# RWKV preparation: both heads of a pair in one vector operation, pair products and transposes on quarters of the TensorE array

## The chip, the cores and the metric

The kernel runs on one core of one Trainium2 chip. The metric is the device time of one execution in microseconds (us), lower is better. The time before is the median of three runs. One further execution was profiled; all rows below come from it. "ns" is said where nanoseconds are meant.

## What is computed

One layer of a streaming encoder over 512 tokens of width 1024, in fp32: a pre-norm, one combined input projection `w_in`, two mixers side by side (an RWKV-7 mixer with 8 heads of 64 channels and a gated delta-rule mixer, GDN, with 4 heads of 128), sigmoid gates, an output projection, and a gated MLP of 2816 channels with a short causal convolution. The part around the change is the RWKV mixer. Its recurrence, per head and token, is

```python
sa = jnp.einsum('bhvk,bhk->bhv', S, a_t)
S = S * w_t[:, :, None, :] + sa[..., None] * b_t[:, :, None, :] + v_t[..., None] * k_t[:, :, None, :]
y = jnp.einsum('bhvk,bhk->bhv', S, r_t)
```

The kernel does it in chunks of 64 tokens. With decayed factors a, r (from the left) and b, k (from the right) of a chunk, it needs for each head and chunk the four products b·a, b·r, k·a, k·r, each 64 by 64 and masked to the lower triangle, and b and k themselves turned from channels-by-tokens to tokens-by-channels.

## The kernel before

Activations lie as channels on 128 partitions and 512 tokens in the free direction. A dense projection is done per unit of 128 output columns: `unit` loads 512 KB of weights, ACT writes their rounded part `hi` (line 161), DVE or POOL the remainder `lo` (line 163), and `mm3` issues three matmuls for each of the 8 input blocks (lines 176, 177, 179). These are called dense matmuls below; there are 24 in a unit.

`mixing` walks the list `ORDER`. `R0` to `R3` prepare the RWKV heads in pairs (`rwkv_prep`, head pair hp: head 2hp on partitions 0 to 63, called lo, head 2hp+1 on 64 to 127, called hi). `i0`, `i1` invert the triangular matrices of two pairs (`rwkv_inverse`), `c0`, `c1` run their chunks (`rwkv_chain`, `rwkv_out`). `a`, `G`, `z`, `I`, `C` are the same for GDN. `g0` to `g13` are dense gate projections that depend on nothing but the normalized input. The order of `ORDER` is a priority: a scheduler (tile pools, semaphores and the order on each engine are made by it when the program is built) takes on each engine the first piece of work that it believes to be ready. On the chip every engine then runs its own list strictly in that order.

`rwkv_prep` forms the decays `ep`, `em`, then on DVE:

- lines 470 and 472 write a and r: the lo half into the tile `ase`, the hi half into `aso`, each for all 8 chunks (64 partitions x 512);
- lines 486 and 491 write b and k into two tiles `BK`, one for each half of the sequence (4 chunks), per head and half: 4 + 4 operations of 64 partitions x 256. For the lo head b lies in slot 0 and k in slot 1, for the hi head the other way round;
- line 493 forms r·k·r_k, line 495 sums it on PE ("bones" matmul), line 496 makes `yf` of it.

Then, for each half of the sequence, three PSUM banks are taken (`pe`, `po`, `pt`). Lines 505 and 506 multiply, per chunk, the 64 rows of one head against [a r] into all 128 columns: the lo head into `pe`, the hi head into `po`. fp32 matmuls are issued twice, so a call in the code is two instructions in the trace. Line 508 transposes `BK` on the whole array into `pt`. DVE masks the products out of PSUM (line 512, four operations of 64 partitions x 512 for each half) into `ntb`, `ase`, `aso`; ACT copies `pt` (line 515); DVE scales `ntb` (line 516).

All PSUM tiles named `A` come out of one ring of 3 banks (`bank`, `BANKS`): the fourth `A` waits until the first has been read. `A` serves line 495, the products, the transposes, and several others.

`rwkv_inverse` begins on PE with line 569, after the last of 64 dependent DVE operations and the transpose of line 547.

## Time and profile before

| | |
|---|---|
| median of 3 runs | 902.66 us (899.92 to 904.11) |
| profiled execution | 901.19 us |
| its span, first to last instruction | 899.4 us |
| PE busy | 866.2 us, 96% |
| DVE busy | 590.1 us, 66% |
| ACT, POOL busy | 464.0 us, 195.4 us |
| granted TensorE clock | 0.992 of full speed |

The profile names an instruction by line, engine and operation, with the tiles that it writes and reads (`R` is the tile that holds `ase`, `aso`, `ntb`, `bkt`; `A`, `B`, `D` are PSUM banks; `P`, `T` work tiles). PE is the matrix engine, DVE the vector engine, ACT the scalar engine. A matmul's recorded duration includes the pipeline behind it; how fast PE proceeds is read from the distance of two starts. The first 48 us load inputs and form the first tiles, the mixing stage lies between some 48 and 433 us, projections and the MLP fill the rest.

### The profile page before, as it was taken

How to read it: one execution, taken by the hardware profiler on the slowest of the kernel's cores; microseconds unless marked ns; L12 is line 12 of the kernel's file. 1: busy time of each engine (PE TensorE's matmuls, PEld its weight loads, DVE VectorE, ACT ScalarE, POOL GpSimd, SP SyncE). 2: the span in 40 equal slices, each digit the busy share in tenths (PEclk: the TensorE clock that was granted, in tenths of full speed). 3: DMA queues.
4: the chain of work that ended last, by engine and by line, in shares of the span. 5: the costliest groups of instructions: out<-in, count | busy, mean ns of one | idle time of the engine just before them, and what ended most of it. 6: DMA issues, size and time to landing. Idle time of an engine off the chain costs nothing.

```text
span 899.4 us, 13124 instructions
## 1 busy us (share of the span) xinstructions
PE 866.2 (96%) x4925; PEld 675.9 (75%) x4925; DVE 590.1 (66%) x1156; ACT 464.0 (52%) x879; POOL 195.4 (22%) x182
## 2 busy tenths in 40 slices
PE   7998999999999999999999999999999999999995
PEld 4776777666767777677787888888888888888885
DVE  6799797874888987855486448766666666312125
ACT  7654457667443776583534464444444444323233
POOL 2241123111121221111222213222222222222221
PEclk8999999999999999999999999999999999999998
DMA  6331222121212221135252223332223333223234
GB/s 238 119 105 60 71 71 72 48 72 48 71 59 71 71 72 36 60 113 181 94 188 94 94 76 111 95 94 94 94 94 94 99 103 96 88 88 105 89 106 136
DMA packets 28737, 84.76 MB, mean 94 GB/s; under 512 B 3200, under 2 KB 5376, under 8 KB 28672
## 3 DMA queue, kind: packets, MB, share of 16 engines
q1 hardware_dynamic: 28672, 83.91, 29.3%
q8 instruction: 39, 0.64, 0.3%
q14 instruction: 26, 0.21, 0.1%
HBM read 78.13 MB, written 5.77 MB: 93 GB/s over the span
## 4 chain that ended last, share of the span: by engine, by line
PE 73%; DVE 16%; ACT 4%; issue 3%; DMA 2%; POOL 1%; SPq 0%; DVEq 0%; POOLq 0%; ACTq 0%
PE D L179 20%; PE D L176 20%; PE D L177 20%; DVE R L512 1%; PE A L176 1%; PE A L177 1%; PE A L179 1%; DVE invN L541 1%; DVE lo L163 1%; DVE P L747 1%; DMA raw<-w_in 1%; DVE invY L543 1%; ACT hi L161 1%; DVE R L926 1%; PE B L639 1%
## 5 line engine op out<-in xcount | busy, mean ns | idle before, releaser
L163 POOL TENSOR_TENSOR lo<-raw,hi 128x512 fp32r<-128x512 f32 x133 | 179.8, 1352 | 649.7 <-ACT hi L161 625.8
L161 ACT ACTIVATE hi<-raw 128x512 fp32r<-128x512 f32 (+1 forms) x266 | 165.0, 622 | 257.3 <-PE D L179 193.5
L176 PE MATMUL D<-uh,lo 128*128 128x512 f32 (+1 forms) x456 | 184.0, 405 | 2.7 <-ACT uh L200 1.9
L177 PE MATMUL D<-uh,hi 128*128 128x512 f32 (+1 forms) x456 | 184.1, 405 | 0.0
L163 DVE TENSOR_TENSOR lo<-raw,hi 128x512 fp32r<-128x512 f32 (+1 forms) x133 | 92.4, 695 | 77.2 <-ACT hi L161 76.8
L176 PE MATMUL D<-u2h,lo 128*128 128x512 f32 x352 | 137.9, 392 | 0.0
L177 PE MATMUL D<-u2h,hi 128*128 128x512 f32 x352 | 137.8, 392 | 0.0
L179 PE MATMUL D<-ul,hi 128*128 128x512 f32 (+1 forms) x456 | 135.4, 403 | 0.4 <-DVE ul L198 0.4
L176 PEld LDWEIGHTS D<-uh,lo 128*128 128x128 f32 x456 | 86.2, 189 | 23.5 <-ACT uh L200 2.4
L177 PEld LDWEIGHTS D<-uh,hi 128*128 128x128 f32 x456 | 86.1, 189 | 18.8 <-issue 1.0
L179 PEld LDWEIGHTS D<-ul,hi 128*128 128x128 f32 x456 | 82.6, 188 | 19.6 <-issue 1.2
L179 PE MATMUL D<-u2l,hi 128*128 128x512 f32 x352 | 95.1, 392 | 0.0
L177 PEld LDWEIGHTS D<-u2h,hi 128*128 128x128 f32 x352 | 66.1, 188 | 14.9 <-issue 0.2
L176 PEld LDWEIGHTS D<-u2h,lo 128*128 128x128 f32 x352 | 66.1, 188 | 14.7 <-issue 0.2
L179 PEld LDWEIGHTS D<-u2l,hi 128*128 128x128 f32 x352 | 66.1, 188 | 14.1
L972 DVE SCALAR_TENSOR_TENSOR P<-T,vecs,P 128x511 f32<-128x511 f32 x88 | 69.0, 784 | 8.9 <-ACT P L970 2.8
L969 DVE TENSOR_TENSOR T<-D,acc 128x512 f32<-128x512 f32 x44 | 30.3, 690 | 49.8 <-PE D L179 45.8
L177 PE MATMUL D<-ah,hi 128*128 128x512 f32 (+1 forms) x126 | 45.2, 366 | 0.0
L176 PE MATMUL D<-ah,lo 128*128 128x512 f32 (+1 forms) x126 | 45.1, 366 | 0.0
L541 DVE TENSOR_TENSOR invN<-invA,invY 128x60 f32<-128x60 f32 (+24 forms) x124 | 33.2, 268 | 2.6
L543 DVE TENSOR_TENSOR invY<-invY,invN 128x60 f32<-128x60 f32 (+24 forms) x124 | 32.9, 266 | 2.9
L970 ACT ACTIVATE P<-T,vecs 128x512 f32<-128x512 f32 x44 | 31.8, 723 | 5.4 <-DVE T L969 1.9
(342 smaller groups left out, 1280.1 us busy)
## 6 DMA issues: line engine op xcount, KB each, us to landing
raw<-w_in SPq DMA_DIRECT2D x44, 512.0 KB, 3.6
raw<-ffn_up SPq DMA_DIRECT2D x44, 512.0 KB, 3.5
raw<-ffn_down SPq DMA_DIRECT2D x18, 512.0 KB, 3.5
raw<-w_out SPq DMA_DIRECT2D x8, 512.0 KB, 3.5
spill<-T SPq DMA_DIRECT2D x14, 256.0 KB, 2.0
R<-spill SPq DMA_DIRECT2D x14, 256.0 KB, 5.6
raw<-ffn_down SPq DMA_DIRECT2D x9, 384.0 KB, 3.0
xin<-xT SPq DMA_DIRECT2D x8, 256.0 KB, 5.7
```

The lines of the kernel that those rows point to most:

```text
L161: nc.scalar.activation(hi[:, 0:w], raw[:, o:o + w], AF.Copy)
L163: self.on(str(self.halves % 4)).tensor_tensor(out=lo[:, 0:w], in0=raw[:, o:o + w], in1=hi[:, 0:w].bitcast(F32), op=ALU.subtract)
L176: nc.tensor.matmul(ps, wl[:, w[k]], x[k][0], start=(first and i == 0 and k == 0), stop=False)
L177: nc.tensor.matmul(ps, wh[:, w[k]], x[k][0], start=False, stop=False)
L179: nc.tensor.matmul(ps, wh[:, w[k]], x[k][1], start=False, stop=(last and i == len(parts) - 1 and k == n - 1))
L512: nc.vector.tensor_tensor(out=tl[s, w].rearrange("p c s t -> p c (s t)"), in0=ps[s, :].rearrange("p (c t) -> p c t", c=4), in1=rwm[s].unsq ...
L541: nc.vector.tensor_tensor(out=w, in0=rows[:, t, 0:t].unsqueeze(2).broadcast_to([128, t, n]), in1=Ym[:, t, c:G].unsqueeze(1).broadcast_to([ ...
L543: nc.vector.tensor_tensor(out=Ym[:, 0:t, c:G], in0=Ym[:, 0:t, c:G], in1=w, op=ALU.add)
L639: nc.tensor.matmul(pz[lo, 0, i, :], R[hp]["ase"][:, c, 0, :], se[:, i, 0, :], start=True, stop=True)
L969: nc.vector.tensor_tensor(out=h, in0=ps, in1=self.acc2, op=ALU.mult)
L970: nc.scalar.activation(cv, h, AF.Copy, scale=w(2))
L972: nc.vector.scalar_tensor_tensor(out=cv[:, sh:], in0=h[:, 0:T - sh], scalar=w(2 - sh), in1=cv[:, sh:], op0=ALU.mult, op1=ALU.add)
```

## The change

In `rwkv_prep` alone (two other places follow the new shape of the `BK` buffer, which is one tile of double size now in place of two):

- a and r are written for both heads by one operation each, into `ase` on all 128 partitions. ACT copies the hi half into `aso` afterwards, in two pieces.
- b and k are written for both heads and all 8 chunks by one operation each, b in slot 0 and k in slot 1 for both heads.
- A product is split into quarters of the array: 64 rows of one head against [a r] into 64 columns. Per chunk there are four: lo and hi head with b into the bank `pn` (lo into partitions 0 to 63, hi into 64 to 127), lo and hi head with k into the bank `pq` (halves crossed). The two banks thus hold roles (all b products, all k products), not heads, and two heads write one bank.
- `pn` is masked by one operation of 128 partitions, `pq` by two of 64: three for each half of the sequence, not four.
- The transposes are fp32 matmuls of a quarter against a 64 by 64 identity, 32 calls for 8 of before, at the end, into two banks for the whole sequence.

```diff
-        zero = self.work.tile([128, T], BF16, tag="BK", name="zero", bufs=2)
+        zero = self.work.tile([128, 2 * T], F32, tag="BK", name="zero", bufs=1).bitcast(BF16)[:, 0:T]
...
-        for tl, s in ((ase, slice(0, 64)), (aso, slice(64, 128))):
-            nc.vector.scalar_tensor_tensor(out=tl[s, :, 0, :], in0=kv[s], scalar=self.nkk[s, hp:hp + 1], in1=ep[s, :, 0:64],
-                                           op0=ALU.mult, op1=ALU.mult)
-            self.on("e").tensor_tensor(out=tl[s, :, 1, :], in0=rv[s], in1=ep[s, :, 1:65], op=ALU.mult)
+        lo, hi = slice(0, 64), slice(64, 128)
+
+        nc.vector.scalar_tensor_tensor(out=ase[:, :, 0, :], in0=kv, scalar=self.nkk[:, hp:hp + 1], in1=ep[:, :, 0:64],
+                                       op0=ALU.mult, op1=ALU.mult)
+        self.on("e").tensor_tensor(out=ase[:, :, 1, :], in0=rv, in1=ep[:, :, 1:65], op=ALU.mult)
+        for h in range(2):
+            nc.scalar.activation(aso[hi, 4 * h:4 * h + 4], ase[hi, 4 * h:4 * h + 4], AF.Copy)
...
-        bkh = [self.work.tile([128, 4, 2, 64], F32, tag="BK", name=self.nm("BK"), bufs=2) for _ in range(2)]
-        q = lambda x, s, h: x[s, h * 256:h * 256 + 256].rearrange("p (c t) -> p c t", c=4)
-        for h in range(2):
-            for s, sb in ((slice(0, 64), 0), (slice(64, 128), 1)):
-                nc.vector.scalar_tensor_tensor(out=bkh[h][s, :, sb, :], in0=q(K, s, h), scalar=self.hkk[s, hp:hp + 1],
-                                               in1=q(at, s, h), op0=ALU.mult, op1=ALU.mult)
+        bk = self.work.tile([128, 8, 2, 64], F32, tag="BK", name=self.nm("BK"), bufs=1)
+        c8 = lambda x: x.rearrange("p (c t) -> p c t", c=8)
+        nc.vector.scalar_tensor_tensor(out=bk[:, :, 0, :], in0=kv, scalar=self.hkk[:, hp:hp + 1], in1=c8(at),
+                                       op0=ALU.mult, op1=ALU.mult)
         self.on("b").tensor_tensor(out=K, in0=K, in1=tha, op=ALU.mult)
-        for h in range(2):
-            for s, sk in ((slice(0, 64), 1), (slice(64, 128), 0)):
-                self.on("c").tensor_tensor(out=bkh[h][s, :, sk, :], in0=q(K, s, h), in1=q(em, s, h), op=ALU.mult)
+        self.on("c").tensor_tensor(out=bk[:, :, 1, :], in0=kv, in1=c8(em), op=ALU.mult)
...
+        ident = self.con("ident")
+        quarters = ((lo, lo, 0), (hi, hi, 0), (lo, hi, 1), (hi, lo, 1))
         for h in range(2):
-            pe, po, pt = self.bank(), self.bank(), self.bank()
+            pn, pq = self.bank(), self.bank()
             for c in range(4):
...
-                nc.tensor.matmul(pe[:, o], bk[0:64], ase[0:64, cc].rearrange("p s t -> p (s t)"), start=True, stop=True)
-                nc.tensor.matmul(po[:, o], bk[64:128], aso[64:128, cc].rearrange("p s t -> p (s t)"), start=True, stop=True)
-            for c in range(4):
-                nc.tensor.transpose(pt[:, c * 128:c * 128 + 128], bkh[h][:, c, :, :].rearrange("p s t -> p (s t)"), self.con("ident"))
+                cc, o = 4 * h + c, slice(c * 128, c * 128 + 128)
+                for r_, w_, sl in quarters:
+                    nc.tensor.matmul((pn, pq)[sl][w_, o], bk[r_, cc, sl, :], ase[r_, cc].rearrange("p s t -> p (s t)"),
+                                     start=True, stop=True)
             w = slice(4 * h, 4 * h + 4)
-            for ps, s, tl in ((pe, lo, ntb), (pe, hi, ase), (po, hi, ntb), (po, lo, aso)):
+            for ps, s, tl in ((pn, slice(0, 128), ntb), (pq, hi, ase), (pq, lo, aso)):
...
-            nc.scalar.activation(bkt[:, w, :], pt.rearrange("p (c t) -> p c t", c=4), AF.Copy)
+        pt = [self.bank() for _ in range(2)]
+        for c in range(8):
+            for r_, w_, sl in quarters:
+                f = r_.start
+                nc.tensor.matmul(pt[f // 64][w_, c * 64:c * 64 + 64], bk[r_, c, sl, :], ident[r_, f:f + 64], start=True, stop=True)
+        for i in range(2):
+            nc.scalar.activation(bkt[:, :, 64 * i:64 * i + 64], c8(pt[i]), AF.Copy)
```

In the changed kernel the masks stand on line 511, the transposes on 518, the products on 507, the factors on 472, 474, 488 and 491; later lines move by 5.

The scheduler lays out the mixing stage anew. Three places follow, first before, then with the change.

PE at R0's products. In these rows `A_..` are the banks of the ring (the first number), `BK_..` the b/k tile, `R_27` the pair's `ase` or `aso`, `D_..` rows dense matmuls. Before:

```order
L179 MATMUL D_105_654<-ul_76,hi_103_650 128x512 x4
L495 MATMUL A_78_523<-P_29_277,cons_70 128x512
L505 MATMUL A_79_526<-R_27_275,BK_76_511 128x128
L506 MATMUL A_80_527<-R_27_275,BK_76_511 128x128
...
L176 MATMUL D_130_785<-uh_75,lo_127_778 128x512
L177 MATMUL D_130_785<-uh_75,hi_126_777 128x512
L176 MATMUL D_130_785<-uh_75,lo_127_778 128x512
L508 MATMUL A_81_528<-cons_70,BK_76_511 128x128 x4
...
L505 MATMUL A_82_546<-R_27_275,BK_77_512 128x128
L506 MATMUL A_83_547<-R_27_275,BK_77_512 128x128
...
L508 MATMUL A_84_548<-cons_70,BK_77_512 128x128 x4
```

With the change:

```order
L177 MATMUL D_104_685<-uh_75,hi_102_681 128x512
L495 MATMUL A_77_516<-P_29_277,cons_70 128x512
L507 MATMUL A_78_519<-R_27_275,BK_76_511 64x128 x2
L507 MATMUL A_79_520<-R_27_275,BK_76_511 64x128 x2
...
L507 MATMUL A_80_540<-R_27_275,BK_76_511 64x128 x5
L507 MATMUL A_81_541<-R_27_275,BK_76_511 64x128 x4
...
L518 MATMUL A_82_561<-cons_70,BK_76_511 64x64 x9
L518 MATMUL A_83_562<-cons_70,BK_76_511 64x64 x9
...
L176 MATMUL D_104_685<-uh_75,lo_103_682 128x512
```

Line 495 moved ahead of 8 dense matmuls of its unit; no dense matmul stands any more between it and the last transpose (before, 7 did in R0, 4 in R1 and R2, 2 in R3). `A_81` is the fourth ring bank after `A_78`, `A_82` after `A_79`, `A_83` after `A_80`.

DVE in R0, from the b/k factors to the masks. Before:

```order
L486 SCALAR_TENSOR_TENSOR BK_76_511<-P_28_276,sp_245,T_75_508 64x4x64 x2
L163 TENSOR_TENSOR lo_129_782<-raw_125_775,hi_128_781 128x512
L486 SCALAR_TENSOR_TENSOR BK_77_512<-P_28_276,sp_245,T_75_508 64x4x64 x2
L488 TENSOR_TENSOR P_28_276<-P_28_276,T_74_506 128x512
L491 TENSOR_TENSOR BK_76_511<-P_28_276,T_70_484 64x4x64 x2
L491 TENSOR_TENSOR BK_77_512<-P_28_276,T_70_484 64x4x64 x2
L493 SCALAR_TENSOR_TENSOR P_29_277<-P_29_277,vecs_69,P_28_276 128x512
...
L496 TENSOR_TENSOR yf_80<-A_78_523,R_27_275 128x512
L512 TENSOR_TENSOR R_27_275<-A_79_526,cons_70 64x512 x2
L512 TENSOR_TENSOR R_27_275<-A_80_527,cons_70 64x512 x2
```

With the change:

```order
L488 SCALAR_TENSOR_TENSOR BK_76_511<-P_28_276,sp_245,T_75_508 128x8x64
L163 TENSOR_TENSOR lo_127_844<-raw_123_837,hi_126_843 128x512
L490 TENSOR_TENSOR P_28_276<-P_28_276,T_74_506 128x512
L491 TENSOR_TENSOR BK_76_511<-P_28_276,T_70_484 128x8x64
L493 SCALAR_TENSOR_TENSOR P_29_277<-P_29_277,vecs_69,P_28_276 128x512
L351 SCALAR_TENSOR_TENSOR P_86_600<-D_98_648,vecs_69,P_86_600 128x511
L496 TENSOR_TENSOR yf_80<-A_77_516,R_27_275 128x512
L511 TENSOR_TENSOR R_27_275<-A_78_519,cons_70 128x512
L511 TENSOR_TENSOR R_27_275<-A_79_520,cons_70 64x512 x2
L511 TENSOR_TENSOR R_27_275<-A_80_540,cons_70 128x512
L511 TENSOR_TENSOR R_27_275<-A_81_541,cons_70 64x512 x2
```

Eight operations on b and k became two, the masks of `pn` are one operation, and the masks follow `yf` without a stop, in the order in which PE wants the banks back.

PE at the first matmul of the first inverse, i0 (`G_190` is the tile of G1, `G_153` with the change that of G0). Before:

```order
L770 MATMUL A_208_1390<-cons_70,G_190_1301 128x128 x4
...
L176 MATMUL D_230_1504<-uh_75,lo_229_1501 128x512
L177 MATMUL D_230_1504<-uh_75,hi_228_1500 128x512
L569 MATMUL B_153_1028<-invA_151_950,R_27_275 32x32 x16
L569 MATMUL B_153_1028<-invA_151_950,R_85_567 32x32 x16
```

With the change (lines moved by 5):

```order
L791 MATMUL A_182_1320<-cons_70,T_181_1318 128x128 x4
L803 MATMUL A_185_1334<-G_153_1170 128x128 x3
L574 MATMUL B_151_1090<-invA_149_1012,R_27_275 32x32 x16
L574 MATMUL B_151_1090<-invA_149_1012,R_84_598 32x32 x16
L803 MATMUL A_185_1334<-G_153_1170 128x128
```

The inverse's first matmul stood behind the transposes of G1 (line 770) and stands inside G0's preparation now: 448 dense matmuls of the program are ahead of it before, 378 with the change. The DVE operations of G1 that stood ahead of it went behind it.

## Rows read from the trace of the kernel before

**Rows 1.** The page: the span, the busy time of each engine, and the chain of work that ended last, by engine.

```profile
span 899.4 us, 13124 instructions
PE 866.2 (96%) x4925; PEld 675.9 (75%) x4925; DVE 590.1 (66%) x1156; ACT 464.0 (52%) x879; POOL 195.4 (22%) x182
PE 73%; DVE 16%; ACT 4%; issue 3%; DMA 2%; POOL 1%; SPq 0%; DVEq 0%; POOLq 0%; ACTq 0%
```

**Rows 2.** Busy time by stretches: 20 us with a preparation (R1), 2 us out of them, and 20 us in the MLP. Columns: stretch, its length, busy us (and count) of PE, weight loads, DVE, ACT, POOL, then granted clock, DMA share, GB/s.

```profile
80.00:100.00 20.00, 18.71 (x100) 14.04 (x99) 16.84 (x29) 8.11 (x15) 3.61 (x5) 0.91 0.24 79
...
86.00:88.00 2.00, 2.00 (x6) 1.62 (x5) 1.92 (x6) 1.45 (x3) 0.18 (x1) 0.50 0.26 102
...
540.00:560.00 20.00, 20.00 (x89) 16.39 (x89) 17.40 (x22) 8.88 (x16) 5.79 (x4) 1.00 0.31 96
```

**Rows 3.** The waits of PE: which instruction waited for which, us in total, times, longest.

```profile
PE A L495 <- DVE P L493: 3.2, 3, 1.9
PE A L770 <- DVE G L751: 1.5, 2, 1.0
PE B L651 <- ACT SUV L648: 1.5, 3, 0.7
PE A L460 <- ACT T L456: 1.1, 1, 1.1
PE A L799 <- ACT T L793: 1.0, 2, 0.6
PE B L569 <- DVE invA L547: 1.0, 2, 0.8
PE A L786 <- POOL T L783: 0.9, 1, 0.9
PE B L881 <- DVE st L895: 0.9, 1, 0.9
PE B L576 <- ACT invY L572: 0.8, 1, 0.8
```

**Rows 4.** Instructions grouped by line and shape: out and in, shapes, count, busy us, mean ns of one, idle time before them.

```profile
L470 DVE SCALAR_TENSOR_TENSOR R<-P,sp,Ep 64x512 f32<-64x512 f32 x8 | 6.2, 772 | 2.0 <-ACT Ep L450 1.9
L472 DVE TENSOR_TENSOR R<-P,Ep 64x512 f32<-64x512 f32 x8 | 5.7, 710 | 0.0
L486 DVE SCALAR_TENSOR_TENSOR BK<-P,sp,T 64x256 f32<-64x256 f32 x16 | 8.6, 540 | 0.2
L491 DVE TENSOR_TENSOR BK<-P,T 64x256 f32<-64x256 f32 x16 | 8.7, 544 | 0.2
L512 DVE TENSOR_TENSOR R<-A,cons 64x512 f32<-64x512 f32 x32 | 21.1, 686 | 1.4 <-PE A L506 1.1
L493 DVE SCALAR_TENSOR_TENSOR P<-P,vecs,P 128x512 f32<-128x512 f32 x4 | 3.0, 752 | 0.1
L496 DVE TENSOR_TENSOR yf<-A,R 128x512 f32<-128x512 f32 x4 | 2.7, 687 | 2.2 <-PE A L495 2.2
L515 ACT ACTIVATE R<-A 128x512 f32<-128x512 f32 x8 | 4.8, 599 | 22.1 <-PE A L508 22.1
```

**Rows 5.** PE in order of time around the products of R0, R1 and R3: start us, us, instruction, count, and in brackets the idle time ahead of it. For each, line 495 and the first matmul behind the last transpose; for R0 also the first product and the first matmul behind the first 16 products.

```profile
69.89 1.13 PE L495 MATMUL A<-P,cons 128*128 128x512 f32 x2 [1.85 <-DVE P L493]
70.95 0.37 PE L505 MATMUL A<-R,BK 64*128 64x128 f32 x1
...
72.04 0.50 PE L176 MATMUL D<-uh,lo 128*128 128x512 f32 x1
...
76.27 0.48 PE L177 MATMUL D<-uh,hi 128*128 128x512 f32 x1
...
94.73 1.13 PE L495 MATMUL A<-P,cons 128*128 128x512 f32 x2
...
100.14 0.94 PE L179 MATMUL D<-ul,hi 128*128 128x512 f32 x3
...
268.85 1.12 PE L495 MATMUL A<-P,cons 128*128 128x512 f32 x2 [1.07 <-DVE P L493]
...
274.34 0.39 PE L881 MATMUL B<-G 128*128 128x128 f32 x2
```

**Rows 6.** PE in order of time where, in the chunk chain c0, two kinds of quarter matmul alternate: line 645 (lo to lo, hi to hi) and lines 626, 627 (lo to hi, hi to lo, both into the one bank `pv`). 64 columns are streamed in each.

```profile
185.18 0.23 PE L645 MATMUL B<-Z,R 64*64 64x64 f32 x2
185.22 0.22 PE L626 MATMUL B<-cons,R 64*64 64x64 f32 x1
185.22 0.22 PE L627 MATMUL B<-cons,R 64*64 64x64 f32 x1
185.24 0.23 PE L645 MATMUL B<-Z,R 64*64 64x64 f32 x2
```

**Rows 7.** PE in order of time at line 460 of R1, and two dense matmuls soon after it (columns as in rows 5).

```profile
84.21 1.05 PE L460 MATMUL A<-cons,T 128*128 128x2 f32 x8 [1.14 <-ACT T L456]
...
87.25 0.63 PE L177 MATMUL D<-uh,hi 128*128 128x512 f32 x1
87.68 0.63 PE L176 MATMUL D<-uh,lo 128*128 128x512 f32 x1
```

**Rows 8.** DVE in order of time behind line 495 of R1 (columns as in rows 5).

```profile
95.90 0.69 DVE L496 TENSOR_TENSOR yf<-A,R 128x512 f32<-128x512 f32 x1 [1.22 <-PE A L495]
96.98 4.61 DVE L512 TENSOR_TENSOR R<-A,cons 64x512 f32<-64x512 f32 x7 [0.39 <-PE A L506]
```

More of the change, by code (lines that the diff above doesn't have):

```diff
@@ L393, in mixing @@
         y = [self.inv(x) for x in "NAY"]
-        y = [t[:, o:o + T] for t in y[:2] for o in (0, T)] + [y[2], self.t("P")] + [self.work.tile([128, T], F32, tag="BK", name=self.nm("BK"), bufs=2) for _ in range(2)]
+        bk = self.work.tile([128, 2 * T], F32, tag="BK", name=self.nm("BK"), bufs=1)
+        y = [t[:, o:o + T] for t in y[:2] for o in (0, T)] + [y[2], self.t("P")] + [bk[:, o:o + T] for o in (0, T)]
         y = [t.bitcast(F32R) for t in y]
@@ L498, in rwkv_prep @@
         rwm = self.con("rwm")
+        ident = self.con("ident")
+        quarters = ((lo, lo, 0), (hi, hi, 0), (lo, hi, 1), (hi, lo, 1))
         for h in range(2):
-            pe, po, pt = self.bank(), self.bank(), self.bank()
+            pn, pq = self.bank(), self.bank()
             for c in range(4):
-                o = slice(c * 128, c * 128 + 128)
-                cc = 4 * h + c
-                bk = bkh[h][:, c, :, :].rearrange("p s t -> p (s t)")
-                nc.tensor.matmul(pe[:, o], bk[0:64], ase[0:64, cc].rearrange("p s t -> p (s t)"), start=True, stop=True)
-                nc.tensor.matmul(po[:, o], bk[64:128], aso[64:128, cc].rearrange("p s t -> p (s t)"), start=True, stop=True)
@@ L507, in rwkv_prep @@
-            for c in range(4):
-                nc.tensor.transpose(pt[:, c * 128:c * 128 + 128], bkh[h][:, c, :, :].rearrange("p s t -> p (s t)"), self.con("ident"))
+                cc, o = 4 * h + c, slice(c * 128, c * 128 + 128)
+                for r_, w_, sl in quarters:
+                    nc.tensor.matmul((pn, pq)[sl][w_, o], bk[r_, cc, sl, :], ase[r_, cc].rearrange("p s t -> p (s t)"),
+                                     start=True, stop=True)
             w = slice(4 * h, 4 * h + 4)
-            lo, hi = slice(0, 64), slice(64, 128)
@@ L511, in rwkv_prep @@
-            for ps, s, tl in ((pe, lo, ntb), (pe, hi, ase), (po, hi, ntb), (po, lo, aso)):
+            for ps, s, tl in ((pn, slice(0, 128), ntb), (pq, hi, ase), (pq, lo, aso)):
                 nc.vector.tensor_tensor(out=tl[s, w].rearrange("p c s t -> p c (s t)"),
                                         in0=ps[s, :].rearrange("p (c t) -> p c t", c=4),
-                                        in1=rwm[s].unsqueeze(1).broadcast_to([64, 4, 128]), op=ALU.mult)
-            nc.scalar.activation(bkt[:, w, :], pt.rearrange("p (c t) -> p c t", c=4), AF.Copy)
+                                        in1=rwm[s].unsqueeze(1).broadcast_to([s.stop - s.start, 4, 128]), op=ALU.mult)
```

## The prediction

> **What bounds the kernel now.** Three views, in this order. The page says that PE is busy for 866.2 of 899.4 us and makes up 73% of the chain that ended last, DVE 16% [rows 1]. PE is the bound, and a change pays only where it takes work off PE or a wait out of PE's list. The stretches show where waits can be: in the MLP PE is busy all the time and starts a dense matmul every 20.00/89 = 0.225 us; in the 20 us around R1 it is busy 18.71 us, while DVE is busy 16.84 [rows 2]. The mixing stage is thus the place, and its DVE is nearly as full as its PE. The list of PE's waits then says for whom: the longest is line 495, the first matmul of a preparation's end, which waited three times for DVE's line 493, 3.2 us in all; the other eight rows that I use (line 460 among them) hold 8.7 us, nearly all for DVE, or for an ACT or POOL step that stands in a chain with it [rows 3]. All nine together are 11.9 us, 1.3% of the time: that is about what a lighter DVE can give back.
>
> **The change, part by part.**
>
> *DVE, factors.* Operations on 64 partitions become operations on 128 with as many elements for each partition. Line 512 (64 partitions x 512) takes 686 ns and line 496 (128 x 512, from the same memory) 687 [rows 4]: height costs nothing. So of each pair on lines 470 and 472 one goes, 0.77 + 0.71 us. The four operations of line 486 (540 ns each) become one at the price of line 493's form, 752 ns: 4 x 0.540 - 0.752 = 1.41 us; line 491 likewise, 4 x 0.544 - 0.752 = 1.42 us [rows 4]. Ahead of line 493 each preparation is 4.3 us shorter on DVE.
>
> *DVE, masks.* Eight operations of 0.69 us become six, 1.3 us less. Per preparation 5.6 us, in all 22.5 us of DVE. None of it counts directly; it counts where PE waited.
>
> *ACT.* Two copies of the hi half per preparation; the nearest row is line 515, 599 ns for 512 elements on each partition [rows 4], so 1.2 us at most. ACT is busy 8.11 of 20 us there [rows 2], and the copies are needed only by the second mask of `pq`, behind eight other DVE operations. Cost nothing; if that cover went, a mask would come up to 1.2 us later.
>
> *PE, work.* Products: 32 calls for 16, each for half the columns. Before, 16 instructions (two heads side by side, four chunks, two passes) took 70.95 to 72.04, 1.09 us, switches of the array's shape included [rows 5]. If all four quarters run at once the new half takes the same 1.09. No row shows this shape with 128 streamed columns, but one shows four quarters with 64: two of line 645, one each of 626 and 627 start within 0.04 us and the next two of line 645 come 0.06 us after the first [rows 6]. That is a step of 0.06 us for four. The bounds are four at a time (no cost) and two at a time (as before: 1.09 us more per half, at most 2.2 per preparation). I take four, by rows 6. The transposes are then 16 steps of 0.06 = 0.95 us.
>
> The Trainium skill speaks against this: its page "TensorEngine Tiling (Array Packing)", section "Restrictions and Gotchas", says that different row tiles cannot access the same PSUM bank at the same time. Lines 626 and 627 read different row halves, write one bank and start together at 185.22 [rows 6], so this trace does not bear it out for quarters with crossed or straight outputs. By the rule the sum would be that of the third rival.
>
> *PE, waits inside the block.* This is the cost. Before, line 495 to the last transpose took 6.38 us in R0 with 7 dense matmuls inside, 5.41 in R1 with 4, 5.49 in R3 with 2 [rows 5]; at 0.225 us for each dense one, PE spent 4.8, 4.5 and 5.0 us on the block itself, about 4.7. Now no dense matmul stands inside, and the banks come round in a ring of three, so PE waits for masks. From the start of line 495: it takes 1.06 [rows 5], the first half's products 1.09, to 2.15. `yf` starts 0.11 after line 495's slot, masks follow 0.1 after the products at 0.66 us each (4.61 us for seven) [rows 8]: the `pn` mask runs 2.25 to 2.91, the two of `pq` to 4.23, the next `pn` mask to 4.89. `A_81` is free at 2.95, so the second half ends near 3.9; `A_82` at 4.27, nine transposes take 0.52; `A_83` at 4.93, nine more to 5.45, the last fourteen in sevens of four to 5.9. So 5.9 us in place of 4.7: +1.2 per preparation, **+4.8 us** in all. Bounds: 4.2 us if banks never held PE (-2.0 in all), 8.1 if quarters went two at a time and nothing of it fell into the waits (+13.6).
>
> *PE, waits that go.* Line 495: DVE reaches line 493 some 4.3 us earlier per preparation, while PE reaches line 495 only 8 x 0.225 = 1.8 us earlier in R0. The longest wait was 1.85 [rows 5]; 1.85 + 1.8 is less than 4.3, so all **-3.2 us** [rows 3] go. Line 460 of R1: 1.14 us of wait, after which the clock fell: dense matmuls start 0.43 us apart, at a granted 0.50, the 1.2 GHz level [rows 2, 7]; 0.09 of the 20 us were lost to it, 1.8 us [rows 2]. R1's chain starts behind R0's DVE work, 5.6 us shorter: **-2.9 us**. The other rows, 7.6 us [rows 3], are inverses, GDN preparations and one chunk chain behind it on DVE. The first inverse now stands 70 dense matmuls earlier, 15.8 us of PE, against 11.2 us that two preparations save; DVE work of G1 that went behind it must give the rest, so this wait may stay. I take two thirds, **-5.0 us**. What is late next on PE is then the masks inside the block.
>
> *BK in one buffer, start and tail.* A preparation writes the buffer in the last operations ahead of line 493; R0's transposes end 18 us before R1's line 495 [rows 5]. Free. The MLP is untouched.
>
> **Sum.** +4.8 - 3.2 - 2.9 - 5.0 = -6.3 us. The profiled execution took 901.19, 1.5 below the median of 902.66; from it 894.9, on the median's scale **896.4 us**. A difference of 0.5%, 4.5 us, is about what a measurement of this kernel can tell from none.
>
> **The rivals.**
>
> 1. *The waits come back.* The new order is as tight as the old one: where DVE has less to do, the scheduler has put PE's step earlier (line 495, the inverse), and waits reappear at other steps. Against it: DVE loses 4.3 us ahead of line 495, the order took 1.8 of them. For it: the inverse moved by more than the preparations save. Then only lines 495 and 460 give: +4.8 - 6.1, 901.4 us; with one or two new waits up to 904.
> 2. *The clock falls at every block: slower.* In R1 a wait of 1.14 us and eight matmuls that stream 2 columns were followed by the 1.2 GHz level [rows 7, 2]. The new block has some 1.9 us of waits in its 5.9 and no dense matmul. If PE's clock is taken down behind each of the four, at 1.8 us each (7.2), and little of the 7.6 goes, the time is 902.7 + 4.8 + 7.2 - 3.2 - 2.9 = 908.6; with two of the 7.6, 906.6. It decides for slower from three of four blocks on. Against it: R0 idled 1.85 us ahead of line 495 [rows 5], and the clock of the whole run is 0.992.
> 3. *Two heads cannot write one bank at once.* Then each half's products go two at a time, +2.2 us per preparation less what falls into the waits, say +7.5: 904.
> 4. *All nine waits go, and the block costs PE what it did before* (the banks hold it less than worked out): -3.2 - 2.9 - 7.6 = -13.7, 889 us.
>
> That the program doesn't do what it says is not likely: the order shows the operations.
>
> **How the numbers follow.** Forecast 0.50 (892 to 899: 0.43 beyond 0.5% faster, 0.07 within); rival 1 0.27 (0.02 faster, 0.25 within); rival 2 0.10 (0.09 slower, 0.01 within); rival 3 0.06 (0.05 within, 0.01 slower); rival 4 0.07, faster. So faster 0.52, same 0.38, slower 0.10. The range reaches from rival 4's 889 over the forecast and rival 1 to rival 3 with 905; rival 2 is left out above.
>
> **What would show it.** Right: DVE's busy time near 567 us; line 495 without a wait; 16 product instructions in steps of four; a block of near 5.9 us with waits on line 511 ahead of lines 507 and 518; no stretch at 0.50 near R1. Wrong: steps of two (rival 3), a clock below 0.95 in the stretches of R0 to R3 (rival 2), waits of lines 574, 775, 804 as large as before (rival 1). If the block took 4.7 us with PE never waiting in it, the term of +4.8 was wrong.

## The result and the profile after

The change is slower: 907.6 us median of 15 runs (904.2 to 911.0) against 901.6 for the kernel before (15 runs, 899.2 to 904.1), ratio 1.0064 with a 95% interval of 1.0048 to 1.0080. The forecast was 896.4, its range ended at 905. The profiled execution took 904.8, span 903.0.

The page of the changed kernel answers to [rows 1]:

```profile
span 903.0 us, 13798 instructions
PE 872.0 (97%) x5277; PEld 683.4 (76%) x5277; DVE 573.7 (64%) x1116; ACT 468.5 (52%) x887; POOL 195.4 (22%) x182
```

DVE lost 16.4 us of work, and PE still was busy 5.8 us longer. The waits of PE, as [rows 3] (lines moved by 5; line 460 is 461 now, 569 is 574, 770 is 775):

```profile
PE B L574 <- DVE invA L552: 3.0, 2, 1.7
PE A L710 <- DVE ab_x L707: 2.3, 1, 2.3
PE A L518 <- DVE R L511: 1.7, 4, 0.4
PE A L775 <- DVE G L756: 0.9, 1, 0.9
PE A L495 <- DVE P L493: 0.5, 1, 0.5
PE B L656 <- ACT SUV L653: 0.4, 1, 0.4
PE A L461 <- ACT T L457: 0.3, 1, 0.3
PE A L804 <- ACT T L798: 0.2, 1, 0.2
```

Lines 495 and 461 hardly wait any more. In their place stand the first inverse (line 574) and line 710, the first matmul of the GDN gates, which did not wait before. Behind line 574 the granted clock falls to 0.50, the 1.2 GHz level. Stretches as [rows 2]: R1's block, and two after i0's first matmul at 132.53:

```profile
86.00:88.00 2.00, 1.45 (x4) 0.30 (x2) 0.90 (x2) 1.12 (x2) 0.00 (x0) 1.00 0.19 73
...
134.00:136.00 2.00, 2.00 (x9) 1.04 (x7) 0.00 (x0) 1.93 (x4) 0.00 (x0) 0.62 0.00 0
...
138.00:140.00 2.00, 2.00 (x20) 1.94 (x15) 0.56 (x2) 1.57 (x5) 1.07 (x6) 0.50 0.05 12
```

PE around R1's products, as [rows 5]. From 86.96 to 93.17 there is no dense matmul; the waits inside are those for masks:

```profile
86.96 1.12 PE L495 MATMUL A<-P,cons 128*128 128x512 f32 x2 [0.55 <-DVE P L493]
88.01 1.74 PE L507 MATMUL A<-R,BK 64*64 64x128 f32 x42
90.07 1.09 PE L507 MATMUL A<-R,BK 64*64 64x128 f32 x22 [0.31 <-DVE R L511]
91.58 1.65 PE L518 MATMUL A<-cons,BK 64*64 64x64 f32 x64 [0.42 <-DVE R L511]
93.17 0.50 PE L176 MATMUL D<-uh,lo 128*128 128x512 f32 x1
```

Why line 710 waits is seen on DVE, in order of time; line 535 opens the chain of i0's inverse, line 707 feeds the gates:

```profile
95.96 1.25 DVE L535 STREAM_TRANSPOSE invA<-invN 128x1024 f32<-128x1024 f32 x1 [1.91 <-ACT invN L564]
97.31 1.05 DVE L546 TENSOR_TENSOR invN<-invA,invY 128x31 f32<-128x31 f32 x1
...
102.90 1.22 DVE L546 TENSOR_TENSOR invN<-invA,invY 128x115 f32<-128x115 f32 x1
104.04 0.21 DVE L707 TENSOR_TENSOR ab_x<-ab_w,ab_x 128x64 fp32r<-128x64 f32 x1
```

and on PE:

```profile
101.67 0.40 PE L176 MATMUL D<-uh,lo 128*128 128x512 f32 x1
104.40 2.01 PE L710 MATMUL A<-uh,ab_x 128*32 128x512 f32 x8 [2.33 <-DVE ab_x L707]
```

The same two instructions on DVE in the kernel before:

```profile
103.58 0.23 DVE L702 TENSOR_TENSOR ab_x<-ab_w,ab_x 128x64 fp32r<-128x64 f32 x1
105.92 1.25 DVE L530 STREAM_TRANSPOSE invA<-invN 128x1024 f32<-128x1024 f32 x1 [2.12 <-ACT invN L559]
```

The chain of i0 starts 10 us earlier than before (95.96 against 105.92), and line 707, which stood ahead of the chain, now stands behind its 18th operation. Line 707 runs when line 702 ran (104.04 against 103.58), but PE, with as many dense matmuls ahead of it as before (301), is through with them some 2 us earlier. Two of the 18 operations, at 97.31 and 102.90, took 1.05 and 1.22 us where the other operations of lines 546 and 548 between them took 0.2 to 0.3. POOL worked beside both (last section):

```profile
97.03 1.29 POOL L163 TENSOR_TENSOR lo<-raw,hi 128x512 fp32r<-128x512 f32 x1 [11.34 <-ACT hi L161]
102.63 1.35 POOL L163 TENSOR_TENSOR lo<-raw,hi 128x512 fp32r<-128x512 f32 x1 [4.31 <-ACT hi L161]
```

By these rows the two cost some 1.8 us of the 2.33 that line 710 waits. No run was made without them.

### The profile page after: what moved, and what is told of

Same layout as the page of the kernel before. It is cut to its first block, busy times and chain, and to the rows that moved or that the text cites. A ratio compares the mean times of both kernels' runs of the same rounds, so it can differ in the third digit from the quotient of the medians.

```text
span 903.0 us, 13798 instructions
## 1 busy us (share of the span) xinstructions
PE 872.0 (97%) x5277; PEld 683.4 (76%) x5277; DVE 573.7 (64%) x1116; ACT 468.5 (52%) x887; POOL 195.4 (22%) x182
## 4 chain that ended last, share of the span: by engine, by line
PE 81%; DVE 12%; ACT 3%; issue 2%; DMA 1%; POOL 0%; SPq 0%; DVEq 0%; ACTq 0%; POOLq 0%
PE D L179 21%; PE D L177 21%; PE D L176 21%; DVE invY L548 2%; PE A L176 1%; PE A L177 1%; PE A L179 1%; DVE invN L546 1%; DVE lo L163 1%; DVE P L752 1%; DVE R L511 1%; DVE R L931 1%; PE B L644 1%; PE A L518 1%; ACT hi L161 1%
```

## Where the time goes: one sum for all kernels

The kernels below are read by one sum. The stage runs from the 151st to the 1027th of the 3,138 dense matmuls (in the changed kernel from 47.9 to 406.1 us). *Blocks* is line 495 (or what stands for it) to the first matmul behind the last product or transpose, dense matmuls inside taken off at 0.225 us, all four preparations together. *Idle* is the time outside the blocks in which no matmul ran. *Half clock* adds up length times (1 - granted clock) over stretches of 2 us. *Rest* is what is left. Each line is one profiled execution; the median beside it is that of all its timed runs. The stage is not the whole time: its start alone lies between 47.9 and 49.5 us in two executions of the change.

| kernel | stage us | blocks | idle | half clock | rest | median us |
|---|---|---|---|---|---|---|
| before | 353.2 | 18.9 | 15.5 | 1.7 | 317.1 | 901.6 |
| the change | 358.2 | 24.2 | 12.4 | 3.4 | 318.2 | 907.6 |
| the change, another execution (after_again) | 360.3 | 24.2 | 11.8 | 6.9 | 317.4 | 909.4 |
| factors | 349.5 | 19.0 | 11.8 | 0.0 | 318.6 | 895.8 |
| ar | 352.9 | 18.8 | 15.0 | 1.7 | 317.4 | 900.4 |
| qprod | 363.2 | 21.0 | 18.4 | 4.7 | 319.1 | 915.1 |
| qtrans | 364.8 | 28.3 | 15.1 | 5.1 | 316.2 | 908.2 |
| i0_g1 | 359.3 | 24.2 | 14.5 | 1.7 | 318.9 | 905.8 |
| q_ag3 | 356.5 | 24.8 | 10.1 | 3.4 | 318.2 | 902.4 |
| ag3_i0g1 | 356.7 | 24.8 | 13.1 | 0.0 | 318.9 | 902.7 |
| f_ag3 | 352.8 | 19.0 | 13.4 | 1.7 | 318.7 | 899.4 |
| b_ag3 | 356.9 | 20.0 | 19.6 | 1.7 | 315.6 | 904.1 |
| qprod_ord | 364.5 | 21.0 | 16.5 | 8.5 | 318.5 | 912.5 |
| q_tfirst | 357.7 | 24.1 | 15.3 | 1.7 | 316.6 | 905.5 |
| f_tfirst | 353.8 | 24.7 | 10.8 | 1.7 | 316.6 | 901.0 |
| f_t2 | 356.6 | 24.8 | 13.0 | 0.0 | 318.8 | 902.6 |
| f_t3 | 367.6 | 29.8 | 16.4 | 1.7 | 319.8 | 914.3 |
| q_not | 363.5 | 15.9 | 19.7 | 9.9 | 318.0 | 912.2 |

The rest is the same within 2.5 us of 318 in all of them, while the stage moves by 18. A least-squares fit over the 18 lines gives 1.02 us of stage for each us of blocks, 0.96 for idle time and 0.99 for half clock, and leaves a scatter of 1.1 us. So blocks, idle time and half clock account for the differences, each paid about one for one; between two single lines the rest can differ by 4 us. This is a reading of traces: no run changed one of the three and left the others.

## The experiments: the parts of the change apart

Two theories stood against each other: the *block* (products and transposes without a dense matmul in them), and the *order* (waits and half clock that the new order of steps brings).

### factors

```diff
-                for r_, w_, sl in quarters:
-                    nc.tensor.matmul((pn, pq)[sl][w_, o], bk[r_, cc, sl, :], ase[r_, cc]..., ...)
+                for ps, r_ in ((pe, lo), (po, hi)):
+                    nc.tensor.matmul(ps[:, o], bk[r_, cc]..., ase[r_, cc]..., ...)
...
+            for ps, i, s, tl in ((pe, lo, lo, ntb), (pe, hi, hi, ase), (po, lo, hi, ntb), (po, hi, lo, aso)):
...
+            for c in range(4):
+                nc.tensor.transpose(pt[:, c * 128:c * 128 + 128], bk[:, 4 * h + c]..., ident)
+            nc.scalar.activation(bkt[:, w, 0:64], pv[:, :, 0:64], AF.Copy)
+            nc.scalar.activation(bkt[hi, w, 64:128], pv[lo, :, 64:128], AF.Copy)
+            nc.scalar.activation(bkt[lo, w, 64:128], pv[hi, :, 64:128], AF.Copy)
```

> Factors of both heads in one vector operation as in the change, but products and transposes on PE as before (64 rows by 128 columns, whole-array transposes in each half, 4 dense matmuls between the halves). Block theory (the loss is the block of products and transposes without a dense matmul in it, 6.05 us against 4.7): it gives back 4 x 1.35 = 5.4 us, 902.2. Order theory (the loss is i0's first matmul at dense matmul 378 in place of 448, with its wait of 1.7 us, the wait of 2.3 us at line 710 and some 3.4 us of half clock behind it): i0 stands at 405 here, 6 us later, so the wait of 1.7 and the half clock go, 902.5. Both: 897.

Measured: 895.8 us, ratio 0.9943 (0.9931 to 0.9955), the fastest kernel of the study and better than both others. PE around R1's products:

```profile
87.00 1.16 PE L507 MATMUL A<-R,BK 64*128 64x128 f32 x16
88.09 0.66 PE L516 MATMUL A<-cons,BK 128*128 128x128 f32 x4
88.51 0.48 PE L176 MATMUL D<-uh,lo 128*128 128x512 f32 x1
...
89.66 1.50 PE L507 MATMUL A<-R,BK 64*128 64x128 f32 x16
```

That is near the 897 expected if both theories hold. Four dense matmuls cover the masks again, the block costs what it cost before (19.0 for 18.9), and no stretch of the stage is at half clock. With this list of steps the vector half of the change is worth 5.5 us against the kernel before in the same series (901.2); the matrix half costs 11.8, the difference of the two medians. By the table that is 5.2 of block, up to 0.6 of idle time and 3.4 to 6.9 of half clock. Both halves had their order made anew, so each figure holds an effect of the order.

### qprod and qtrans

qprod keeps the quarter products and has whole-array transposes; qtrans the reverse. The pieces are those of the diff above.

> As the change, but the transposes on the whole array, one bank for each half; 1 dense matmul between the halves, i0 at dense matmul 379. Block theory: the transposes take 0.5 us for each half in place of 1.6 us for both, bank waits stay; 4 x 0.6 = 2.4 less than the change, 905. Order theory: i0 stands where it stood, 907 to 908.

> As the change, but the products on rows as before (lo head in one bank, hi head in the other, 4 dense matmuls inside the block), transposes on quarters; i0 at dense matmul 380. Block theory: dense matmuls fill the waits for banks, some 1.3 us for each preparation, 902.5. Order theory: i0 stands where it stood, 907 to 908, with the wait of line 574 (2 times, 3 us) and the half clock behind it.

Measured: qprod 915.1 us (1.0163, 1.0148 to 1.0178), qtrans 908.2 (1.0086, 1.0073 to 1.0099). Both theories missed qprod by 7 to 10 us: its blocks are shorter than the change's (21.0 for 24.2), but it idles 18.4 us, and has half clock behind line 847 near 402 us. qtrans came out near the 907 to 908 of the order theory, but not for its reason: by the table its blocks cost 4.1 us more than the change's, which that theory did not have. In qtrans dense matmuls do stand in the block, as the block theory wanted, but singly and in pairs among 24, 8 and twice 32 small ones, and the blocks take 28.3. One thing qprod shows cleanly, with the first half's products undisturbed:

```profile
66.51 1.10 PE L507 MATMUL A<-R,BK 64*64 64x128 f32 x32
67.56 0.66 PE L516 MATMUL A<-cons,BK 128*128 128x128 f32 x4
```

32 quarter instructions take 1.05 us; before, 16 row instructions took 1.09 [rows 5]. A step of four quarters, two heads writing one bank, takes what a step of two row instructions took.

### ar

```diff
-        for tl, s in ((ase, slice(0, 64)), (aso, slice(64, 128))):
-            nc.vector.scalar_tensor_tensor(out=tl[s, :, 0, :], ...)
+        nc.vector.scalar_tensor_tensor(out=ase[:, :, 0, :], ...)
...
+            nc.scalar.activation(aso[hi, 4 * h:4 * h + 4], ase[hi, 4 * h:4 * h + 4], AF.Copy)
```

> The kernel before with the a and r factors alone made by one operation each for both heads and copied by ACT (1.48 us less on DVE in each preparation, ahead of line 493); b and k, products and transposes as before, i0 at dense matmul 448 as before. If a lighter DVE pays at line 495 and line 460: their waits of 3.2 and 1.1 us fall by 1.3 each time, some 3 us, and up to 1.8 us of half clock in R1: 896.5 to 899. If not: 901.

Measured: 900.4 us, 0.9990 (0.9976 to 1.0003): nothing that can be told. Two of its waits of PE (line 497 is the bones matmul here, 788 a matmul of the GDN preparation):

```profile
PE A L497 <- DVE P L495: 3.4, 3, 1.3
PE A L788 <- POOL T L785: 2.2, 2, 1.8
```

R0's wait fell from 1.85 to 1.3, R2's grew, and line 788 waits 1.3 us more than its like did before (0.9, [rows 3]). 1.5 us less of DVE ahead of a wait did not take 1.5 us off it, and the 896.5 to 899 us expected if it did are refuted.

## The experiments: the order

### i0_g1, q_ag3, ag3_i0g1

The change with nothing but the list of steps altered: i0 later, the GDN gates (`a`) earlier, both.

```diff
-ORDER = "R0 g0 R1 g1 g2 g3 a i0 G0 G1 z1 ..."
+ORDER = "R0 g0 R1 g1 g2 g3 a G0 G1 i0 z1 ..."   i0_g1
+ORDER = "R0 g0 R1 g1 g2 a g3 i0 G0 G1 z1 ..."   q_ag3
+ORDER = "R0 g0 R1 g1 g2 a g3 G0 G1 i0 z1 ..."   ag3_i0g1
```

> The change with i0 put behind G0 and G1 in the list of steps: its first matmul stands at dense matmul 432 in place of 378, all else ahead of it (the blocks too) as in the change. Block theory: nothing changes, 907 to 908. Order theory: the wait of 1.7 us ahead of i0's first matmul and the half clock behind it (3.4 us) go, 902.5; the wait of line 710 (2.3 us) stays.

> The change with the GDN gates ahead of g3, and i0 where the change has it (dense matmul 378). Order theory: the wait of 2.3 us at the ab matmul goes, the wait at i0 and the half clock behind it stay: 907.6 - 2.3 = 905.3, 2 to 3 us above the kernel with both steps moved (902.7). Block theory: 907 to 908.

> The change with two steps moved in the list: the GDN gates (ab matmul) ahead of g3, and i0 behind G0 and G1. The DVE operation that feeds the ab matmul stands ahead of the inverse's chain again. Block theory: 907 to 908, as the change, or 905.8 as with i0 alone moved. Order theory: with i0 alone moved 1.8 us were won; now the wait of 2.3 us at the ab matmul goes too, 903.5.

Measured: i0_g1 905.8 us (1.0057, 1.0044 to 1.0069), q_ag3 902.4 (1.0011, 0.9999 to 1.0023), ag3_i0g1 902.7 (1.0018, 1.0008 to 1.0028). Moving i0 took 1.7 us of half clock and put a wait of 2.9 us at line 804 in its place. Moving the gates alone gave 5.2 us, more than the 2.3 of its wait, and with the gates moved, moving i0 as well gave nothing. In q_ag3, DVE and then PE:

```profile
90.06 0.22 DVE L707 TENSOR_TENSOR ab_x<-ab_w,ab_x 128x64 fp32r<-128x64 f32 x1
```

```profile
94.47 2.00 PE L710 MATMUL A<-uh,ab_x 128*32 128x512 f32 x8 [0.37 <-DVE R L511]
...
131.06 1.20 PE L574 MATMUL B<-invA,R 32*32 32x32 f32 x64
```

Line 707 runs ahead of the chain, line 710 waits 0.37 us in place of 2.33, and i0's first matmul, at the same place of the list, finds its input ready: the wait of 1.7 us and the half clock behind it are gone too (a stretch behind i1's line 574, near 318 us, came instead). The order theory had expected those to stay. So a move of one step, with no operation changed, takes some 5 of the 6 us away. The order of the whole stage is made anew by that move; the place of line 707, an operation of 0.2 us, is the part of it that the rows show. The two profiled executions are only 2.1 us apart (904.8 and 902.7, 2.3 of it idle time), since the change's first profile is one of its fastest (after_again).

### f_ag3 and b_ag3

The same move of the gates in factors, and in the kernel before.

> Factors in one operation, products and transposes as before, with the GDN gates ahead of g3 in the list: the ab matmul at dense matmul 274 in place of 301. It waited 0.6 us with factors alone. Block theory: no change, 895.8. Order theory: the wait goes, 895.2; a gain or loss of over 2 us would mean that the place of one small step carries as much as the whole change.

> The kernel before with one step moved in the list, the GDN gates ahead of g3 (ab matmul at dense matmul 289 in place of 301, i0 at 436 in place of 448); no operation is changed. Block theory: the same time as before, 901 us within 0.5 us. Order theory (waits re-form wherever the order puts a step ahead of its input, and some bring a stretch at half clock): 1 to 4 us away from it, in either direction; with factors alone the same move cost 3.6 us.

Measured: f_ag3 899.4 us (0.9984, 0.9975 to 0.9993), 3.6 slower than factors (where the wait that the expectation puts at 0.6 us is 0.4); b_ag3 904.1 (1.0034, 1.0021 to 1.0046), 3 slower than before, with the same operations. Its waits, to be held against [rows 3]:

```profile
PE A L495 <- DVE P L493: 5.1, 4, 2.0
PE A L770 <- DVE G L751: 3.4, 3, 1.8
```

The move that mends the change spoils the other two. A shift of 3 to 5 us is what the order alone does to this stage.

These runs also allow a comparison of the three kernels under a second list:

| list of steps | before | factors | the change |
|---|---|---|---|
| as it was | 901.6 | 895.8 | 907.6 |
| GDN gates ahead of g3 | 904.1 | 899.4 | 902.4 |

With the second list the change is not slower than the kernel before but 1.7 us faster (the two intervals, 1.0021 to 1.0046 and 0.9999 to 1.0023, just touch), and its matrix half costs 3.0 us, not 11.8. The vector half gains in both lists, 4.7 us in the second. By the table the longer blocks stay in both, 5.2 and 5.8 us against factors; idle time and half clock go with the list. So whether the whole change gains or loses hangs on the order.

### qprod_ord

The list of ag3_i0g1 with qprod.

> Quarter products with whole-array transposes (915.1 us in the change's list of steps), with the GDN gates ahead of g3 and i0 behind G0 and G1. Its block costs 5.25 us against 6.05 in the change. Block theory: 4 x 0.8 less than the change with the same list (902.7), 899.5. Order theory: not to be said beforehand from the block; the half clock at 402 to 413 us and the waits at lines 847 and 791 must go for it to come below 905.

Measured: 912.5 us (1.0127, 1.0111 to 1.0143). The half clock did not go but rose from 4.7 to 8.5 us, at other places. That its shorter block would carry through is refuted; why this kernel meets so much half clock is open.

## The experiments: the length of the block

### q_tfirst and f_tfirst

Transposes ahead of line 493 in place of behind the products, in the change and in factors.

```diff
+        pt = [self.bank() for _ in range(2)]
+        for c in range(8):
+            ...
         nc.vector.scalar_tensor_tensor(out=r, in0=r, scalar=self.vec("r_k", hp), in1=K, op0=ALU.mult, op1=ALU.mult)
```

> The change with the quarter transposes issued ahead of line 493 and the bones matmul in place of behind the products, so that they need no bank that a mask must free, and dense matmuls stand between them and the products; i0 stays at dense matmul 378 and the line that feeds the ab matmul behind the start of the inverse. Block theory (the block of the change costs 6.05 us where before's costs 4.7, 5.4 in all): bank waits of some 1.3 us for each preparation go, 4 x 1.1 = 4.4 less than the change, near 903. Order theory (what is lost sits in the waits at i0 and at the ab matmul and in the half clock behind them): no change, 907 to 908.

> Factors in one operation with products on rows, and the whole-array transposes of both halves ahead of line 493. Block theory: the transposes (0.41 us each half) fill PE while DVE makes line 493, and the second products no longer wait for a bank behind them: up to 4 x 0.5 us less than factors alone (895.8), 894 to 896. Order theory: i0 at 405 as in factors alone, the same time, 895.8.

Measured: q_tfirst 905.5 us (1.0044, 1.0032 to 1.0056), f_tfirst 901.0 (0.9998, 0.9986 to 1.0010). Neither block got shorter: with the transposes counted, q_tfirst's takes 24.1 (24.2 in the change), f_tfirst's 24.7 (19.0 in factors). In f_tfirst the second products wait for the ACT copies of the transposes, 1.7 us in 4 waits, and fewer dense matmuls stand inside. It is 5.3 us slower than factors. That its blocks are 5.7 longer comes near this by luck in part: by the table idle time is 1.0 less, half clock 1.7 more and the rest 2.0 less, and the stage is 4.3 longer.

### f_t2 and f_t3

Factors with each transpose issued two and three times into the same place: a longer block without quarters.

```diff
             for c in range(4):
-                nc.tensor.transpose(...)
+                for _ in range(2):
+                    nc.tensor.transpose(...)
```

> Factors in one operation, products on rows, and each whole-array transpose issued twice into the same place (16 calls more for each preparation's 8, 0.82 us of PE); nothing else changed. 2 dense matmuls stand between the halves, i0 at dense matmul 389. Block theory (time that PE spends in the block is paid one for one): 895.8 + 4 x 0.82 = 899.1. Order theory (longer blocks let the list put i0 earlier, with a wait and a half clock of its own): 1 to 3 us more than that, 900 to 902.

> The same with each transpose issued three times (1.65 us of PE more for each preparation). Hardly a dense matmul is left in the block and i0 stands at 379, the place that it has in the change, though no product and no transpose is on quarters. Block theory: 895.8 + 6.6 = 902.4. Order theory: the waits of the change come with the order (2.3 us at line 710, 1.7 us at line 574, 3.4 us of half clock): 907. If quarters themselves were what costs: 896 to 899.

Measured: f_t2 902.6 us (1.0017, 1.0005 to 1.0029), f_t3 914.3 (1.0133, 1.0113 to 1.0153). More than either theory said. f_t3, R1:

```profile
89.61 1.16 PE L507 MATMUL A<-R,BK 64*128 64x128 f32 x16
90.70 1.53 PE L517 MATMUL A<-cons,BK 128*128 128x128 f32 x12
92.38 1.16 PE L507 MATMUL A<-R,BK 64*128 64x128 f32 x8
...
93.90 1.16 PE L507 MATMUL A<-R,BK 64*128 64x128 f32 x8
```

Blocks of 24.8 and 29.8 us against 19.0, by the table 5.8 of f_t2's 7.1 and 10.8 of f_t3's 18.1. The extra transposes themselves are 3.3 and 6.6 of that. Most of the remainder is in the second products: in the first half the 16 row instructions of the two heads run side by side and take 1.09 us to the next line's start, in the second half the order has the 8 of one head, a dense matmul, and the 8 of the other, and each 8 alone take 1.1 us (in factors the 16 of the second half take 1.4). The rest of f_t3 is 4.6 of idle time (line 710's analogue waits 2.3 again) and 1.7 of half clock. f_t3's i0 stands at 379 with no quarter in it, so the early i0 and the wait at line 710 do not need quarters.

### q_not

```diff
-                nc.tensor.matmul(pt[f // 64][w_, c * 64:c * 64 + 64], bk[r_, c, sl, :], ident[r_, f:f + 64], ...)
...
-            nc.scalar.activation(bkt[:, :, 64 * i:64 * i + 64], c8(pt[i]), AF.Copy)
+            nc.scalar.activation(bkt[:, :, 64 * i:64 * i + 64], bk[:, :, i, :], AF.Copy, scale=0.0)
```

> The change with the transposes left out (what they would give is zero); ACT writes the same tile. The block falls from 6.05 us by some 2.0 to 2.4, i0 stands at 382, the ab matmul behind the start of the inverse as in the change. Block theory alone: 907.6 - 4 x 2.2 = 899. With the order's waits gone besides, 894; with the waits of the change unchanged or larger, 900 or more.

Measured: 912.2 us (1.0123, 1.0094 to 1.0151), 4.6 slower than the change with less work. Its waits of PE at the inverses and at the gates (lines as before the change) and two stretches:

```profile
PE B L569 <- DVE invA L547: 2.9, 2, 1.7
PE A L705 <- DVE ab_x L702: 2.3, 1, 2.3
```

```profile
102.00:104.00 2.00, 2.00 (x6) 0.84 (x5) 1.79 (x7) 0.00 (x0) 0.00 (x0) 0.50 0.19 68
134.00:136.00 2.00, 2.00 (x5) 1.41 (x5) 0.10 (x1) 1.85 (x5) 0.00 (x0) 0.50 0.00 0
```

The block gave 8.3 us; idle time took 7.3 and half clock 6.5 of it (against the change's first profile). The block theory in its plain form (899) falls here. The order theory's "900 or more" holds, but it named no size.

### after_again

> The changed kernel once more, for another profile: its first profiled execution was among the fastest of its runs (904.8 for a median of 907.6, granted clock 0.990 where the median run had 0.986). Order theory: the slower executions have further stretches at half clock at the same waits (lines 710 and 574, the change of stage near 485 us), 1.7 to 3.4 us each. Block theory: the same block, 6.05 us.

Measured: 909.4 us (4 runs); the profiled one took 908.9. The block is the same to 0.01 us, the waits too. But apart from the start and the end, where both profiles have it too, the clock is at its lower level at four places, where the first profile had two of them (behind line 574 and near 487):

```profile
108.00:110.00 2.00, 2.00 (x6) 0.78 (x5) 1.79 (x7) 0.00 (x0) 0.00 (x0) 0.55 0.00 0
...
138.00:140.00 2.00, 2.00 (x6) 0.68 (x4) 0.13 (x1) 1.90 (x5) 0.00 (x0) 0.50 0.00 0
...
322.00:324.00 2.00, 2.00 (x47) 1.64 (x48) 0.00 (x0) 1.94 (x4) 0.00 (x0) 0.50 0.00 0
...
490.00:492.00 2.00, 2.00 (x6) 1.62 (x5) 0.53 (x1) 0.47 (x1) 0.39 (x1) 0.50 0.07 29
```

The first three lie behind line 710 and behind line 574 of i0 and of i1, the waits of the list above; the fourth follows a wait of 1.9 us at line 176 for line 200, which all these kernels have. That is the order theory's expectation, and it fits the median above the first profile: over the 15 runs the granted clock goes from 0.990 (904.2 us) over 0.986 (907.6) to 0.980 (911.0).

## Why the prediction was wrong, step by step

- **DVE's work.** Expected 567 us busy, measured 573.7. The counts were right, some durations not. By line and shape, as [rows 4]:

```profile
L491 DVE TENSOR_TENSOR BK<-P,T 128x512 f32<-128x512 f32 x4 | 3.9, 972 | 0.1
L474 DVE TENSOR_TENSOR R<-P,Ep 128x512 f32<-128x512 f32 x4 | 3.8, 955 | 0.0
L472 DVE SCALAR_TENSOR_TENSOR R<-P,sp,Ep 128x512 f32<-128x512 f32 x4 | 3.7, 934 | 2.2 <-ACT Ep L451 2.2
L488 DVE SCALAR_TENSOR_TENSOR BK<-P,sp,T 128x512 f32<-128x512 f32 x4 | 3.0, 748 | 0.1
```

  Line 488 came out at its price (748 for 752), the others some 0.2 us above theirs, since one of the four of each ran beside POOL (last section): 3.61 us for each preparation in place of 2.99. The operations of lines 546 and 548 in the inverses took 2.8 us more; twelve of them ran beside POOL at 0.8 to 1.3 us each (before, eleven at 0.7 to 1.4). The total did not decide, but two of the twelve lie ahead of line 707 and are most of the wait at line 710 (above).
- **The products.** Four quarters at a time: right (32 instructions in 1.05 us in qprod). The granted clock at the block was 1.00.
- **The block, +4.8.** Measured 6.01, 6.21, 5.93 and 6.04 us against the 5.9 worked out, 24.2 against 18.9 in all: +5.3. Right in mechanism (waits of lines 507 and 518 for line 511) and nearly in size.
- **Line 495, -3.2.** Measured 3.2 to 0.5: right, short of 0.5.
- **Line 460 and the half clock of R1, -2.9.** 1.1 to 0.3, and no stretch near R1 is at 0.50: right where it was looked for. But of the 2.9, 1.8 was half clock, and the term took that for a thing of R1. It went with R1's wait and came back behind others: 1.7 us in the stage before, 3.4 and 6.9 now. The stage has 1.7 to 5.2 us more of it in place of 1.8 less, so this part of the term failed as well.
- **The other waits, -5.0.** This is the main step that failed; the half clock is the other. Six of the seven rows that it rests on did shrink, from 6.6 us in all to 1.5 (line 770, now 775, from 1.5 to 0.9; line 651, now 656, from 1.5 to 0.4; line 799, now 804, from 1.0 to 0.2; the rows of lines 786 and 576 and that of line 881 for line 895 have no successor). But the seventh, line 574, rose from 1.0 to 3.0, line 710 appeared with 2.3, and smaller waits make up the rest. Idle time outside the blocks fell by 3.1 us in all, less than the 3.5 that lines 495 and 461 gave: the other waits together gave nothing. What failed is not the size of the old waits but that the term had no new ones. I had seen that the inverse moved by 15.8 us of PE against 11.2 saved, and still priced the group as if the order were that of before; and I had not looked at what stood behind the inverse on DVE.
- **The sum.** With +5.3, -3.1 and +1.7 of half clock (3.4 for 1.7) the first profile's stage is 3.9 longer, 5.0 with the change of the rest; with the second profile's half clock (6.9) it is 7.1 longer. The medians differ by 6. Against the forecast's -6.3, the first profile's +5.0 is 11.3 more: 5.4 of it are the other waits, 3.5 the half clock, 0.5 the block, 0.8 lines 495 and 460, 1.1 the rest.
- **The rivals.** Rival 1 (the waits come back) names the mechanism, for the reason it gives, and stops at 904, since it has no half clock in it. Rival 2 has the right price of a half-clock stretch (1.8; measured 1.7, and 3.4 for a long one), in the wrong place: at none of the four blocks, but behind the new waits. Rival 3 is refuted by the row of qprod: two at a time would have taken twice the 1.05 us. Rival 4 did not come. The rule of the Trainium skill, page "TensorEngine Tiling (Array Packing)", section "Restrictions and Gotchas", that different row tiles cannot access one PSUM bank at the same time, is not borne out by that row for quarters that write different halves of a bank's partitions.

Shown by experiment: that the vector half alone is faster, in two lists; that the matrix half costs time in both, 11.8 us in one and 3.0 in the other; that some 5 us of the loss go when one step moves. Read from the traces: that the block costs 5 to 6 us more in both lists, and that blocks, idle time and half clock are paid about one for one. Argued only, from the orders: that the number of matrix instructions in the block makes the scheduler put i0 early (f_t3 supports it), and that POOL's work is most of the wait at line 710. Not tried: the quarters with dense matmuls between them at an otherwise unchanged order, since every edit has the order made anew. Open: why the same wait is followed by a half-clock stretch in one execution and not in another.

## What to carry to other kernels

Where a scheduler makes the order anew, an edit is worth its own work on the bounding engine, which can be read off the trace, plus a change of waits that comes out of the new order: look there for the first instruction behind each long chain that moved, on the waiting engine's supplier too, and price it before any "two thirds of the old waits". Hold the effect against what a move of one step without any edit does (here 3 to 5 us), and test the halves of a change apart, under more than one order: the half that takes work off the engine with slack was worth 5.5 and 4.7 us, the half on the bounding engine cost 11.8 and 3.0. A wait can cost more than itself: here waits of 0.9 to 2.9 us were followed by half clock in some executions and not in others, and each such stretch cost 1.7 to 5.1 us.

## What the runs showed of the hardware

- **The clock fell behind the same wait in some executions only.** In the change's two profiles line 710 waited 2.3 us; the stretch 106 to 108 us was granted 1.00 in the first, and 0.59 in the second, where the eight matmuls behind it took 3.1 us from the first start to the next line's. What differs between the two is not to be seen in PE's work, which is the same. The Trainium skill, page "TensorE: Matmul & The Clock Gate", section "What's actually happening", says of a kernel's start that the number of slow matmuls varies from run to run; these runs show the like in the middle of a kernel.
- **DVE beside POOL.** R1's line 491 took 1.82 us where its like take 0.69. DVE, and POOL in the same time:

```profile
84.42 1.82 DVE L491 TENSOR_TENSOR BK<-P,T 128x512 f32<-128x512 f32 x1
```

```profile
84.40 1.28 POOL L163 TENSOR_TENSOR lo<-raw,hi 128x512 fp32r<-128x512 f32 x1 [4.81 <-ACT hi L161]
```

  DVE's operation started 0.02 us behind POOL's and ended 0.56 behind its end, so most of it ran when POOL was done. The Trainium skill, page "SBUF — State Buffer", section "SBUF: two separate sides", says that a DVE operation with two SBUF inputs and a GpSimd operation that reads SBUF shut each other out, and the later one waits; this trace agrees, with 1.13 us.
